# A hybrid mixer block: RWKV recurrence without GpSimd, retention and Mamba products on the full array, another order of issue

## The chip, the cores and the metric

The kernel runs on one core of a Trainium2 chip. The metric is device time in microseconds (us) of one execution; the median of three runs before the change is 1616.52 us (1614.81 to 1617.13).

## What is computed

One layer over 512 tokens and 1024 channels, in float32: `x = x + Mixer(RMSNorm(x))`, `x = x + ConvFFN(RMSNorm(x))`, and a last RMSNorm. The mixer projects the normed input once and feeds four token mixers (Mamba-2, RG-LRU, retention, RWKV-7), gates and projects each, sums them and projects the sum. The three parts that the change touches are, cut to their cores:

```
# RWKV-7, 16 heads of 64, one step per token
sk    = einsum('bhvk,bhk->bhv', state, kk_t)
state = state * w_t - sk * b_t + v_t * k_t
o_t   = einsum('bhvk,bhk->bhv', state, r_t)

# retention, 8 heads, qk width 64, v width 128, chunks of positions
scores  = einsum(q, k) * inner_decay
y_inner = einsum(scores, v)
kv      = einsum(k, v, decay_to_end)        # state that a chunk adds
y_cross = einsum(q * decay_from_start, previous_state)

# Mamba-2, per group of 4 heads
y_diag = einsum(cb * decay, xdt)
```

## The kernel before

Every large product is done three times: `split` cuts a float32 operand into a rounded part (`whi`, `hh`) on ScalarE and a rest (`wlo`, `hl`) on VectorE, and `mm3` (L118 to L121) adds hi*hi, lo*hi and hi*lo in PSUM. A weight block of 128x1024 comes by DMA (`wraw`), is split (`wsplit`), and `proj` or `proj_tokens` multiplies it with all 512 tokens. These blocks are the bulk of the work of TensorE. The small products inside the four mixers are plain float32 matmuls; TensorE does each of these as two passes, and the trace has a row for each pass.

RWKV goes in 8 blocks `j` of two heads. `rwkv_a1(j)` projects r, k and v and makes the decays `dx` and `di`. `rwkv_a2(j)` builds, for 8 chunks of 64 tokens, the stationary operands `g` and `bk` (L354 to L358), multiplies them (L372), masks the result into `g`, `gb` and `ab` (L374 to L376), scales `bk` by the chunk's decay (L381) and transposes it into `bt`, puts `v` into one half of `sv`, and inverts a triangular matrix by a loop of small VectorE operations (L424, L426), with several transfers through DRAM. `rwkv_b(j)` finishes the inverse `tt` (L452 to L465) and runs the recurrence over the 8 chunks:

```
sd = sv[h, c, e] * dl                      # L477, GpSimd, the decayed state
ps = g[c]^T sv[c]                          # L480
pp[c] = ps                                 # L482, VectorE
sk = tt[c]^T pp[c]                         # L484
sv[0:64, c, 0], sv[64:128, c, 1] = sk      # L485 ScalarE, L486 VectorE: solved rows over the state
sk[:, P:] = bt[c]^T sv[c]                  # L488
sv[h, c + 1, e] = sk[...] + sd             # L491, VectorE
```

After the chunks come the outputs (L497 to L501), the head norm (L504 to L517) and the gate; L524 makes the block's last result, which goes to DRAM as `y_dr[3][j]`.

The other three mixers are Python generators (`lru_tiles`, `ret_pair`, `mamba_group`), joined by `filler()` in the order `ORDER`, and behind them three of the four branch projections (`branch` with m = 1, 2, 0). The main loop calls `fill(24.0)` behind each `rwkv_a2(j)` and `fill(43.0)` behind each `rwkv_b(j)`: each takes steps of the generators until their stated us are used up. So a long chain of small RWKV steps stands between dense projections. Behind them come the RWKV branch (`branch(3, 3, merged)`, which needs all of `y_dr[3]`), the output projection and the FFN.

This order of the source is a priority only. The framework's scheduler lays down ahead of the run in which order each engine issues its instructions; it plays the program through a timing model, and an instruction of lower priority goes first where the model has it ready first. Each engine then issues in that fixed order and waits wherever the head of its queue is not ready. A pool with `bufs=n` hands out n buffers of a name; a further tile of that name waits until an older one is done with.

Of the kernel before, what the change touches and what calls it, by code (L numbers as in the profile page):

```python
# [63 lines left out]
def tile_hybrid_block(ctx, tc, x, wts, wzdt, lora, lruw, cpack, consts, rettab, nfin, out):  # L64
# [281 lines left out]
    def rwkv_a2(j, prep):  # L346
# [5 lines left out]
        for e in range(2):  # L352
            h = slice(64 * e, 64 * e + 64)
            nc.gpsimd.tensor_tensor(out=bk[h, :, 1 - e, :], in0=v3(k)[h], in1=v3(di)[h], op=ALU.mult)  # L354
            nc.vector.scalar_tensor_tensor(out=g[h, :, e, e, :], in0=v3(kk)[h], scalar=-1.0, in1=dx[h, :, 0:CH],
                                           op0=ALU.mult, op1=ALU.mult)
            nc.vector.scalar_tensor_tensor(out=bk[h, :, e, :], in0=v3(a)[h], scalar=0.5, in1=v3(di)[h], op0=ALU.mult, op1=ALU.mult)
            nc.gpsimd.tensor_tensor(out=g[h, :, e, 1 - e, :], in0=v3(r)[h], in1=dx[h, :, 1:], op=ALU.mult)  # L358
        nc.vector.scalar_tensor_tensor(out=r, in0=r, scalar=col("rwkv_r_k", j), in1=k, op0=ALU.mult, op1=ALU.mult)
# [20 lines left out]
        bkf = bk.rearrange("p c u t -> p c (u t)")  # L380
        nc.gpsimd.tensor_tensor(out=bkf, in0=bkf, in1=dl.unsqueeze(2).broadcast_to([P, NCH, P]), op=ALU.mult)  # L381
        bt = rkb.tile([P, NCH, P], F32, name="bt")
        for c4 in range(2):
# [3 lines left out]
            nc.scalar.copy(out=bt[:, 4 * c4:4 * c4 + 4, :], in_=ps.rearrange("p (c t) -> p c t", c=4))  # L387
        sv = rkb.tile([P, NCH, 2, 64], F32, name="sv")
        ps = ra.tile([P, S], F32, name="ra")
        for i in range(NT):  # L390
# [3 lines left out]
        for e in range(2):  # L394
            o = slice(64 - 64 * e, P - 64 * e)
            nc.scalar.copy(out=svv[o, :, 0, e], in_=pv[0:64, :, e])
            nc.vector.tensor_copy(out=svv[o, :, 1, e], in_=pv[64:128, :, e])


# [31 lines left out]
        for q in range(4):  # L431
            nc.sync.dma_start(out=xd[:, :, 8 * q:8 * q + 8], in_=xr[32 * q:32 * q + 16])
            nc.sync.dma_start(out=xtd.rearrange("b (m r) i -> b r m i", r=4)[:, q], in_=xt[32 * q:32 * q + 32])
        x11 = rkb.tile([P, NCH, 32], F32, name="x11")
        xtv = xtd.rearrange("(u q) c j -> u c q j", u=2)
        for e in range(2):
            b = 64 * e
            nc.sync.dma_start(out=x11[b:b + 32], in_=xd[8 * e:8 * e + 8].rearrange("q j c -> j q c"))
            for u in range(2):
                w = slice(b + 32 * u, b + 32 * u + 32)  # L440
                nc.sync.dma_start(out=tt[w, :, w], in_=xtv[u][:, 8 * e:8 * e + 8, :])
        return ab, x11, sv, bt, dl, bv

    def rwkv_b(j, held):
        ab, x11, sv, bt, dl, bv = held
        gh, gl = lora_x[2:]
# [20 lines left out]

        o = rkb.tile([P, NT, 2, 64], F32, name="o")
        pp = rkb.tile([P, NCH, 2, 64], F32, name="nt")
        for e in range(2):  # L470
            nc.gpsimd.memset(sv[64 * e:64 * e + 64, 0, e], 0.0)
        for c in range(NCH):
            if c < NCH - 1:
                sd = rkb.tile([P, 64], F32, name="sd", bufs=2)
                for e in range(2):
                    h = slice(64 * e, 64 * e + 64)
                    nc.gpsimd.tensor_scalar(out=sd[h], in0=sv[h, c, e], scalar1=dl[h, c:c + 1], scalar2=None, op0=ALU.mult)  # L477
            ps = rb.tile([P, S], F32, name="rb")
            for e in range(2):
                nc.tensor.matmul(ps[:, e * 64:(e + 1) * 64], g[:, c, e].rearrange("p u t -> p (u t)"), sv[:, c, e, :],  # L480
                                 start=True, stop=True)
            nc.vector.tensor_copy(out=pp[:, c], in_=ps[:, 0:P].rearrange("p (e v) -> p e v", e=2))  # L482
            sk = rb.tile([P, S], F32, name="rb")
            nc.tensor.matmul(sk[:, 0:P], tt[:, c, :], pp[:, c].rearrange("p e v -> p (e v)"), start=True, stop=True)  # L484
            nc.scalar.copy(out=sv[0:64, c, 0], in_=sk[0:64, 0:64])  # L485
            nc.vector.tensor_copy(out=sv[64:128, c, 1], in_=sk[64:128, 64:128])  # L486
            if c < NCH - 1:
                nc.tensor.matmul(sk[:, P:2 * P], bt[:, c, :], sv[:, c].rearrange("p e v -> p (e v)"), start=True, stop=True)  # L488
                for e in range(2):
                    h = slice(64 * e, 64 * e + 64)  # L490
                    nc.vector.tensor_tensor(out=sv[h, c + 1, e], in0=sk[h, P + 64 * e:P + 64 * e + 64], in1=sd[h], op=ALU.add)  # L491
        ppv = pp.rearrange("p (i o) e v -> p i o e v", o=2)
        for n in range(2):
            ps = rb.tile([P, S], F32, name="rb")
            for i in range(NT):
                c = 2 * i + n
                nc.tensor.matmul(ps[:, i * P:(i + 1) * P], gb[:, c, :], sv[:, c].rearrange("p e v -> p (e v)"), start=True, stop=True)  # L497
            pv = ps.rearrange("p (i e v) -> p i e v", i=NT, e=2)
            for e in range(2):
                h = slice(64 - 64 * e, P - 64 * e)  # L500
                nc.vector.tensor_tensor(out=o[64 * n:64 * n + 64, :, e], in0=pv[h, :, e], in1=ppv[h, :, n, e], op=ALU.add)  # L501
# [28 lines left out]
    def bg(shape):  # L530
        return fl.tile(shape, F32, name="bg", bufs=4)

# [77 lines left out]
    def ret_pair(j):  # L610
        q = sm([P, S])
        k = sm([P, S])
        for kind, t, sc in (("ret_q", q, 1.0), ("ret_k", k, 64.0 ** -0.5)):
            nc.scalar.activation(out=t, in_=proj(kind, j), func=AF.Copy, scale=sc)
# [4 lines left out]
            nc.vector.tensor_tensor(out=t, in0=t, in1=rope[0], op=ALU.mult)  # L619
            nc.vector.tensor_tensor(out=t, in0=t, in1=sw, op=ALU.add)  # L620
        vt = bg([P, NT, 256])

        def put(i, ps):
# [5 lines left out]
        tab = sm([P, S])  # L629
        nc.sync.dma_start(out=tab[:, 0:387], in_=rettab[j])  # L630
        qd = sm([P, NT, P])
        nc.vector.tensor_tensor(out=qd, in0=q.rearrange("p (i t) -> p i t", i=NT),
                                in1=tab[:, 256:384].unsqueeze(1).broadcast_to([P, NT, P]), op=ALU.mult)
        ps = inn.tile([P, S], F32, name="inn")
        for i in range(NT - 1):
            transpose(ps[:, i * P:(i + 1) * P], k[:, i * P:(i + 1) * P])
        kd = sm([P, NT, 2, 64])
        nc.vector.tensor_tensor(out=kd[:, 0:NT - 1], in0=ps[:, 0:384].rearrange("p (i e d) -> p i e d", i=NT - 1, e=2),
                                in1=tab[:, 384:386].unsqueeze(1).unsqueeze(3).broadcast_to([P, NT - 1, 2, 64]), op=ALU.mult)
        ps = inn.tile([P, S], F32, name="inn")  # L640
        for i in range(NT - 1):
            for e in range(2):
                nc.tensor.matmul(ps[64 * e:64 * e + 64, i * P:(i + 1) * P], kd[:, i, e, :], vt[:, i, e * P:(e + 1) * P],
                                 start=True, stop=True)
        kvs = sm([P, NT, P])
        nc.vector.tensor_copy(out=kvs[:, 0], in_=ps[:, 0:P])
        for i in range(1, NT - 1):
            nc.vector.scalar_tensor_tensor(out=kvs[:, i], in0=kvs[:, i - 1], scalar=tab[:, 386:387],
                                           in1=ps[:, i * P:(i + 1) * P], op0=ALU.mult, op1=ALU.add)
        for e in range(2):  # L650
            hd = 2 * j + e
            hs = slice(64 * e, 64 * e + 64)
            ps = inn.tile([P, S], F32, name="inn")
            for i in range(NT):
                w = slice(i * P, (i + 1) * P)
                nc.tensor.matmul(ps[:, w], k[hs, w], q[hs, w], start=True, stop=True)
            sc = sm([P, NT, P])
# [3 lines left out]
            for l in range(NT):  # L661
                w = slice(l * P, (l + 1) * P)
                nc.tensor.matmul(yp[:, w], sc[:, l, :], vt[:, l, e * P:(e + 1) * P], start=True, stop=l == 0)
                if l > 0:
                    nc.tensor.matmul(yp[:, w], qd[hs, l, :], kvs[hs, l - 1, :], start=False, stop=True)
            yv = yp.rearrange("p (l v) -> p l v", l=NT)
# [66 lines left out]
    def mamba_group(g):  # L733
# [52 lines left out]
        for i in range(NT):  # L786
            w = slice(i * P, (i + 1) * P)
            yp = inn.tile([P, S], F32, name="inn")
            for h in range(4):
                for u in range(2):  # L790
                    hs = slice(64 * u, 64 * u + 64)
                    nc.tensor.matmul(yp[hs, h * 64:(h + 1) * 64], mts[h][:, i, hs], xdt[:, i, h, :], start=True, stop=True)
            nc.vector.tensor_tensor(out=xs[:, i, :], in0=xs[:, i, :], in1=yp[:, 0:256], op=ALU.add)
# [258 lines left out]
def _shape_constants():  # L1052
# [19 lines left out]
    lg = np.log1p(-np.exp2(-5.0 - np.arange(8)))  # L1072
    tab = np.empty((4, P, 387), np.float64)
    keep = (i[None, :] // CH) >= (i[:, None] // CH)
    for j in range(4):
        for e in range(2):
            h = 2 * j + e
            tab[j, :, e * P:(e + 1) * P] = np.where(keep, np.exp(lg[h] * np.abs(i[None, :] - i[:, None])), 0.0)
            tab[j, 64 * e:64 * e + 64, 256:384] = np.exp(lg[h] * (i + 1.0))
            tab[j, :, 384 + e] = np.exp(lg[h] * (P - 1.0 - i))  # L1080
            tab[j, 64 * e:64 * e + 64, 386] = np.exp(lg[h] * P)
    tab = tab.astype(f)
# [93 lines left out]
```

## Time and profile before

| | |
|---|---|
| median of 3 runs | 1616.52 us (1614.81 to 1617.13) |
| the profiled execution, own time | 1615.14 us |
| its span, first to last instruction | 1613.4 us |
| TensorE busy | 1562.6 us (97%), 8452 matmul passes |
| VectorE, ScalarE, GpSimd busy | 1047.2, 719.7, 141.2 us |
| mean granted TensorE clock | 0.993 of full speed |

Matmuls are pipelined: a pass can start while the one before it is still leaving the array, so the durations of passes overlap, and what a pass costs is read from its start to the next start. A switch to another shape of the array is seen in the same way. PE is TensorE's matmul row, PEld its weight loads, DVE VectorE, ACT ScalarE, POOL GpSimd.

### The profile page before, as it was taken

What the parts mean: (1) busy time and instruction counts of PE and PEld (TensorE: products, weight loads), DVE (VectorE), ACT (ScalarE), POOL (GpSimd) and SP (SyncE); (2) the same over time, 40 slices, a digit from 0 to 9 for tenths busy, and PEclk for the clock granted to TensorE, in tenths of its full rate; (3) what the DMA queues carried; (4) which work ended last, traced back from release to release, by engine and by line L of the source; (5) the groups of instructions that cost most, each with busy time, mean ns of one, the idle gap of its engine ahead of it and who ended that gap; (6) DMA issues with size and microseconds to landing.
All of it is one profiled execution on the core that took longest, in us unless ns stands there. A gap on an engine that the chain in (4) does not pass through costs nothing.

```text
span 1613.4 us, 22510 instructions
## 1 busy us (share of the span) xinstructions
PE 1562.6 (97%) x8452; PEld 1279.7 (79%) x8452; DVE 1047.2 (65%) x2302; ACT 719.7 (45%) x1188; POOL 141.2 (9%) x190
## 2 busy tenths in 40 slices
PE   7899999899999999999999999999999999999998
PEld 7787778787788788877788778788888888888886
DVE  6787697875886788878636757544435665656233
ACT  6453466445753576258422432323223544444122
POOL 1200202202101201201200300100000000000000
PEclk9999999999999999999999999999999999999999
DMA  5233133232243234433533323444222223233231
GB/s 205 92 122 99 56 118 91 76 107 87 87 125 97 77 105 116 125 105 101 163 105 105 118 91 99 133 140 142 91 92 92 94 92 104 91 102 106 95 102 53
DMA packets 108461, 169.47 MB, mean 105 GB/s; under 512 B 54832, under 2 KB 64304, under 8 KB 108352
## 3 DMA queue, kind: packets, MB, share of 16 engines
q1 hardware_dynamic: 107632, 166.92, 33.0%
q8 instruction: 66, 1.08, 0.3%
q10 hardware_dynamic: 720, 1.11, 0.2%
q14 instruction: 43, 0.35, 0.1%
HBM read 150.66 MB, written 15.24 MB: 103 GB/s over the span
## 4 chain that ended last, share of the span: by engine, by line
PE 79%; DVE 14%; ACT 3%; issue 2%; POOL 1%; DMA 1%; SPq 0%; DVEq 0%; ACTq 0%; POOLq 0%
PE acc L119 17%; PE acc L120 17%; PE acc L121 17%; PE acc L949 3%; PE acc L951 3%; PE acc L950 3%; DVE wlo L101 2%; PE rb L480 2%; PE acc L242 2%; PE acc L241 2%; PE acc L240 2%; PE ra L372 1%; PE rb L488 1%; PE inn L96 1%; PE ra L96 1%
## 5 line engine op out<-in xcount | busy, mean ns | idle before, releaser
L119 PE MATMUL acc<-hh,whi 128*128 128x512 f32 (+1 forms) x1240 | 487.3, 393 | 0.0
L120 PE MATMUL acc<-hh,wlo 128*128 128x512 f32 (+1 forms) x1240 | 486.0, 392 | 1.2 <-DVE wlo L101 1.1
L121 PE MATMUL acc<-hl,whi 128*128 128x512 f32 (+1 forms) x1240 | 485.9, 392 | 0.0
L101 DVE TENSOR_TENSOR wlo<-raw,whi 128x1024 fp32r<-128x1024 f32 x228 | 279.1, 1225 | 169.7 <-ACT whi L100 168.8
L100 ACT CAST whi<-raw 128x1024 fp32r<-128x1024 f32 x228 | 237.8, 1045 | 205.9 <-PE acc L951 86.5
L120 PEld LDWEIGHTS acc<-hh,wlo 128*128 128x128 f32 x1240 | 234.3, 189 | 45.6 <-issue 2.2
L119 PEld LDWEIGHTS acc<-hh,whi 128*128 128x128 f32 x1240 | 234.3, 189 | 44.6 <-issue 2.2
L121 PEld LDWEIGHTS acc<-hl,whi 128*128 128x128 f32 x1240 | 234.2, 189 | 44.3 <-issue 1.8
L1004 DVE SCALAR_TENSOR_TENSOR fc<-acc,fw,fc 128x511 f32<-128x511 f32 x88 | 65.9, 749 | 76.5 <-ACT fc L1002 75.0
L119 PE MATMUL acc<-yh,whi 128*128 128x512 f32 x256 | 102.4, 400 | 0.0
L120 PE MATMUL acc<-yh,wlo 128*128 128x512 f32 x256 | 101.1, 395 | 0.0
L121 PE MATMUL acc<-yl,whi 128*128 128x512 f32 x256 | 100.9, 395 | 0.0
L477 POOL TENSOR_SCALAR sd<-sv,dl 64x64 f32<-64x64 f32 x112 | 57.4, 513 | 351.4 <-DVE sv L491 338.0
L1002 ACT ACTIVATE fc<-acc,fw 128x512 f32<-128x512 f32 x44 | 34.3, 779 | 93.9 <-PE acc L121 93.9
L240 PE MATMUL acc<-whi,hh 128*128 128x256 f32 (+1 forms) x256 | 74.8, 293 | 0.4 <-ACT whi L100 0.4
L241 PE MATMUL acc<-wlo,hh 128*128 128x256 f32 (+1 forms) x256 | 74.4, 291 | 0.0
L242 PE MATMUL acc<-whi,hl 128*128 128x256 f32 (+1 forms) x256 | 74.1, 290 | 0.0
L949 PE MATMUL acc<-whi,gh 128*128 128x512 f32 x176 | 69.4, 395 | 0.0
L951 PE MATMUL acc<-whi,gl 128*128 128x512 f32 x176 | 69.4, 395 | 0.0
L950 PE MATMUL acc<-wlo,gh 128*128 128x512 f32 x176 | 69.4, 395 | 0.0
L878 ACT ACTIVATE gt<-acc 128x512 f32<-128x512 f32 x32 | 19.0, 597 | 91.0 <-PE acc L121 91.0
L424 DVE TENSOR_TENSOR prod<-nt,xr 128x60 f32<-128x60 f32 (+24 forms) x248 | 54.0, 218 | 5.5
(329 smaller groups left out, 2404.8 us busy)
## 6 DMA issues: line engine op xcount, KB each, us to landing
raw<-in_wts_dram SPq DMA_DIRECT2D x226, 512.0 KB, 3.3
yr<-y SPq DMA_DIRECT2D x32, 256.0 KB, 2.8
y<-sm SPq DMA_DIRECT2D x24, 256.0 KB, 2.2
nt<-nd SPq DMA_DIRECT2D x32, 128.0 KB, 3.2
sm<-acd SPq DMA_DIRECT2D x16, 256.0 KB, 3.6
x<-in_x_dram SPq DMA_DIRECT2D x4, 512.0 KB, 5.3
ym<-bg SPq DMA_DIRECT2D x16, 128.0 KB, 1.8
sm<-sm SPq DMA_DIRECT2D x32, 64.0 KB, 2.0
```

The lines of the kernel that those rows point to most:

```text
L100: nc.scalar.copy(out=hi, in_=src)
L101: nc.vector.tensor_tensor(out=lo, in0=src, in1=hi.bitcast(F32), op=ALU.subtract)
L119: nc.tensor.matmul(ps, wh, xh, start=first, stop=False)
L120: nc.tensor.matmul(ps, wl, xh, start=False, stop=False)
L121: nc.tensor.matmul(ps, wh, xl, start=False, stop=last)
L240: nc.tensor.matmul(o, hh[:, ko, t], wh[:, s], start=ko == 0, stop=False)
L241: nc.tensor.matmul(o, hh[:, ko, t], wl[:, s], start=False, stop=False)
L242: nc.tensor.matmul(o, hl[:, ko, t], wh[:, s], start=False, stop=ko == KT - 1)
L949: nc.tensor.matmul(ps[i], xh[:, ko, t], w[0][:, s], start=ko == 0, stop=False)
L950: nc.tensor.matmul(ps[i], xh[:, ko, t], w[1][:, s], start=False, stop=False)
L951: nc.tensor.matmul(ps[i], xl[:, ko, t], w[0][:, s], start=False, stop=ko == 2 * nblk - 1)
L1004: nc.vector.scalar_tensor_tensor(out=t[:, s:], in0=ps[:, :S - s], scalar=fw[:, o + 2 - s:o + 3 - s], in1=t[:, s:], op0=ALU.mult, op1=ALU.add)
```

## The change

Recurrence: the solved rows and `v` go into a tile `uv` of their own, `v` being copied from `sv` by GpSimd; `sd` is gone, and the decay is fused into the addition on VectorE. Two multiplications of `rwkv_a2` (of `g` and of `bk`) move from GpSimd to VectorE. `x11` shares the buffer of `xr`, and `o` that of `ab`. Retention: `q` is laid out for both heads with zeros in the other head's 64 partitions (set by GpSimd), so that scores and cross terms contract over 128 partitions, and the keys `kd` are masked per head so that the chunk's state is accumulated by two matmuls of 128 columns. Mamba: two matmuls of 64 columns become one of 128. The pool of large tiles `bg` has 6 buffers in place of 4. The scheduler plays the program through another, finer timing model (`schedule_with_timeline_sim=True`), so the order of issue on every engine is laid down anew.

```
@@ rwkv_a2
-            nc.gpsimd.tensor_tensor(out=g[h, :, e, 1 - e, :], in0=v3(r)[h], in1=dx[h, :, 1:], op=ALU.mult)
+            nc.vector.tensor_tensor(out=g[h, :, e, 1 - e, :], in0=v3(r)[h], in1=dx[h, :, 1:], op=ALU.mult)
...
-        nc.gpsimd.tensor_tensor(out=bkf, in0=bkf, in1=dl.unsqueeze(2).broadcast_to([P, NCH, P]), op=ALU.mult)
+        nc.vector.tensor_tensor(out=bkf, in0=bkf, in1=dl.unsqueeze(2).broadcast_to([P, NCH, P]), op=ALU.mult)
...
+        uv = rkb.tile([P, NCH, 2, 64], F32, name="uv")
...
+            nc.gpsimd.tensor_copy(out=uv[o, :, e], in_=sv[o, :, e])
...
-        x11 = rkb.tile([P, NCH, 32], F32, name="x11")
+        x11 = rkb.tile([P, NCH, 32], F32, name="xr")
@@ rwkv_b
-        o = rkb.tile([P, NT, 2, 64], F32, name="o")
+        o = rkb.tile([P, NT, 2, 64], F32, name="ab")
...
-                sd = rkb.tile([P, 64], F32, name="sd", bufs=2)
-                for e in range(2):
-                    h = slice(64 * e, 64 * e + 64)
-                    nc.gpsimd.tensor_scalar(out=sd[h], in0=sv[h, c, e], scalar1=dl[h, c:c + 1], scalar2=None, op0=ALU.mult)
...
-            nc.scalar.copy(out=sv[0:64, c, 0], in_=sk[0:64, 0:64])
-            nc.vector.tensor_copy(out=sv[64:128, c, 1], in_=sk[64:128, 64:128])
+            nc.scalar.copy(out=uv[0:64, c, 0], in_=sk[0:64, 0:64])
+            nc.vector.tensor_copy(out=uv[64:128, c, 1], in_=sk[64:128, 64:128])
...
-                    nc.vector.tensor_tensor(out=sv[h, c + 1, e], in0=sk[h, P + 64 * e:P + 64 * e + 64], in1=sd[h], op=ALU.add)
+                    nc.vector.scalar_tensor_tensor(out=sv[h, c + 1, e], in0=sv[h, c, e], scalar=dl[h, c:c + 1],
+                                                   in1=sk[h, P + 64 * e:P + 64 * e + 64], op0=ALU.mult, op1=ALU.add)
@@ bg
-        return fl.tile(shape, F32, name="bg", bufs=4)
+        return fl.tile(shape, F32, name="bg", bufs=6)
@@ ret_pair
-        q = sm([P, S])
+        q = bg([P, 2, NT, P])
+        for e in range(2):
+            nc.gpsimd.memset(q[64 - 64 * e:P - 64 * e, e], 0.0)
...
-            nc.vector.tensor_tensor(out=t, in0=t, in1=sw, op=ALU.add)
+                nc.vector.tensor_tensor(out=k, in0=t, in1=sw, op=ALU.add)
+                for e in range(2):
+                    nc.vector.tensor_tensor(out=q[h, e].rearrange("p i t -> p (i t)"), in0=t[h], in1=sw[h], op=ALU.add)
...
-        kd = sm([P, NT, 2, 64])
+        kd = bg([P, 2, NT - 1, 2, 64])
...
-                nc.tensor.matmul(ps[64 * e:64 * e + 64, i * P:(i + 1) * P], kd[:, i, e, :], vt[:, i, e * P:(e + 1) * P],
-                                 start=True, stop=True)
+                nc.tensor.matmul(ps[:, i * P:(i + 1) * P], kd[:, e, i].rearrange("p f d -> p (f d)"), vt[:, i, e * P:(e + 1) * P],
+                                 start=e == 0, stop=e == 1)
...
-                nc.tensor.matmul(ps[:, w], k[hs, w], q[hs, w], start=True, stop=True)
+                nc.tensor.matmul(ps[:, w], k[:, w], q[:, e, i], start=True, stop=True)
...
-                    nc.tensor.matmul(yp[:, w], qd[hs, l, :], kvs[hs, l - 1, :], start=False, stop=True)
+                    nc.tensor.matmul(yp[:, w], qd[:, e, l], kvs[:, l - 1, :], start=False, stop=True)
@@ mamba_group
-                for u in range(2):
-                    hs = slice(64 * u, 64 * u + 64)
-                    nc.tensor.matmul(yp[hs, h * 64:(h + 1) * 64], mts[h][:, i, hs], xdt[:, i, h, :], start=True, stop=True)
+                nc.tensor.matmul(yp[:, h * 64:(h + 1) * 64], mts[h][:, i, :], xdt[:, i, h, :], start=True, stop=True)
@@ kernel
-    with _tile.TileContext(nc) as tc:
+    with _tile.TileContext(nc, schedule_with_timeline_sim=True) as tc:
```

`qd` likewise covers both heads in one operation over 128x1024, and `rettab` has 389 columns in place of 387 for the masks.

## Rows read from the trace of the kernel before

**Rows 1.** The page's busy time: us (share of the span) and instructions, by engine.
```profile
PE 1562.6 (97%) x8452; PEld 1279.7 (79%) x8452; DVE 1047.2 (65%) x2302; ACT 719.7 (45%) x1188; POOL 141.2 (9%) x190
```

**Rows 2.** Busy us by stretch: stretch, its length, then per engine; granted clock, DMA.
```profile
0.00:100.00 100.00, 83.73 (x487) 73.44 (x488) 72.58 (x178) 55.80 (x95) 14.23 (x17) 0.97 0.41 138
1100.00:1613.00 513.00, 505.94 (x2294) 418.08 (x2292) 254.63 (x339) 186.19 (x251) 0.00 (x0) 1.00 0.29 97
```

**Rows 3.** Waits of PE: who waited for whom, us in total, times, longest.
```profile
PE ra L372 <- DVE bk L357: 4.5, 1, 4.5
PE ra L96 <- POOL bk L381: 4.5, 4, 2.3
```

**Rows 4.** Timeline of PE, a burst of 128x128 float32 passes: start, us, what.
```profile
199.82 1.13 PE L372 MATMUL ra<-g,bk 128*128 128x128 f32 x8 [0.52 <-DVE gb L376]
200.71 0.48 PE L119 MATMUL acc<-hh,whi 128*128 128x512 f32 x1
...
201.02 0.40 PE L120 MATMUL acc<-hh,wlo 128*128 128x512 f32 x1
```

**Rows 5.** Timeline of PE, scores and outputs of one retention head.
```profile
702.79 0.39 PE L119 MATMUL acc<-hh,whi 128*128 128x512 f32 x1
703.11 1.16 PE L656 MATMUL inn<-sm 64*128 64x128 f32 x8
704.19 0.50 PE L120 MATMUL acc<-hh,wlo 128*128 128x512 f32 x1
704.53 0.39 PE L121 MATMUL acc<-hl,whi 128*128 128x512 f32 x1
704.76 0.40 PE L119 MATMUL acc<-hh,whi 128*128 128x512 f32 x1
...
705.46 0.61 PE L663 MATMUL inn<-bg,sm 128*128 128x128 f32 x4
...
708.07 0.50 PE L119 MATMUL acc<-hh,whi 128*128 128x512 f32 x1
```

**Rows 6.** Timeline of PE, the states of one retention pair.
```profile
149.55 0.88 PE L643 MATMUL inn<-bg,sm 128*64 128x128 f32 x12
150.36 0.50 PE L121 MATMUL acc<-hl,whi 128*128 128x512 f32 x1
150.69 0.40 PE L119 MATMUL acc<-hh,whi 128*128 128x512 f32 x1
```

**Rows 7.** Timeline of PE, one tile of a Mamba group.
```profile
137.61 0.28 PE L242 MATMUL acc<-whi,hl 128*128 128x256 f32 x1
137.82 0.69 PE L792 MATMUL inn<-bg,sm 128*64 128x64 f32 x16
138.43 0.39 PE L240 MATMUL acc<-whi,hh 128*128 128x256 f32 x1
138.65 0.28 PE L241 MATMUL acc<-wlo,hh 128*128 128x256 f32 x1
138.77 0.28 PE L242 MATMUL acc<-whi,hl 128*128 128x256 f32 x1
```

**Rows 8.** Groups of GpSimd's instructions: busy us, mean ns | idle before, releasers.
```profile
L477 POOL TENSOR_SCALAR sd<-sv,dl 64x64 f32<-64x64 f32 x112 | 57.4, 513 | 351.4 <-DVE sv L491 338.0 <-DVE dx L338 6.1 <-DVE dl L361 1.6
...
L358 POOL TENSOR_TENSOR g<-pr,dx 64x512 f32<-64x512 f32 x16 | 22.0, 1377 | 66.2 <-ACT dx L339 65.2
L381 POOL TENSOR_TENSOR bk<-bk,dl 128x1024 f32<-128x1024 f32 x8 | 16.0, 1996 | 180.0 <-PE ra L372 180.0
```

**Rows 9.** Timeline around the first hand-over of `ab` and `o`.
```profile
196.65 0.81 ACT L374 COPY ab<-ra 64x256 f32<-64x256 f32 x2
...
212.28 0.60 PE L96 MATMUL rb<-ident,o 128*128 128x128 f32 x4
```

**Rows 10.** Timeline of DVE: RWKV's last result; the third branch's last product.
```profile
1057.21 0.69 DVE L524 TENSOR_TENSOR yu<-yu,rb 128x512 f32<-128x512 f32 x1
...
1106.67 0.69 DVE L894 TENSOR_TENSOR gt<-acc,gt 128x512 f32<-128x512 f32 x1 [1.68 <-PE acc L121]
```

More of the change, by code (lines that the diff above doesn't have):

```diff
@@ L441, in rwkv_a2 @@
                 nc.sync.dma_start(out=tt[w, :, w], in_=xtv[u][:, 8 * e:8 * e + 8, :])
-        return ab, x11, sv, bt, dl, bv
+        return ab, x11, sv, uv, bt, dl, bv
     def rwkv_b(j, held):
-        ab, x11, sv, bt, dl, bv = held
+        ab, x11, sv, uv, bt, dl, bv = held
         gh, gl = lora_x[2:]
@@ L472, in rwkv_b @@
         for c in range(NCH):
-            if c < NCH - 1:
-                sd = rkb.tile([P, 64], F32, name="sd", bufs=2)
-                for e in range(2):
-                    h = slice(64 * e, 64 * e + 64)
-                    nc.gpsimd.tensor_scalar(out=sd[h], in0=sv[h, c, e], scalar1=dl[h, c:c + 1], scalar2=None, op0=ALU.mult)
             ps = rb.tile([P, S], F32, name="rb")
@@ L484, in rwkv_b @@
             nc.tensor.matmul(sk[:, 0:P], tt[:, c, :], pp[:, c].rearrange("p e v -> p (e v)"), start=True, stop=True)
-            nc.scalar.copy(out=sv[0:64, c, 0], in_=sk[0:64, 0:64])
-            nc.vector.tensor_copy(out=sv[64:128, c, 1], in_=sk[64:128, 64:128])
+            nc.scalar.copy(out=uv[0:64, c, 0], in_=sk[0:64, 0:64])
+            nc.vector.tensor_copy(out=uv[64:128, c, 1], in_=sk[64:128, 64:128])
             if c < NCH - 1:
-                nc.tensor.matmul(sk[:, P:2 * P], bt[:, c, :], sv[:, c].rearrange("p e v -> p (e v)"), start=True, stop=True)
+                nc.tensor.matmul(sk[:, P:2 * P], bt[:, c, :], uv[:, c].rearrange("p e v -> p (e v)"), start=True, stop=True)
                 for e in range(2):
                     h = slice(64 * e, 64 * e + 64)
-                    nc.vector.tensor_tensor(out=sv[h, c + 1, e], in0=sk[h, P + 64 * e:P + 64 * e + 64], in1=sd[h], op=ALU.add)
+                    nc.vector.scalar_tensor_tensor(out=sv[h, c + 1, e], in0=sv[h, c, e], scalar=dl[h, c:c + 1],
+                                                   in1=sk[h, P + 64 * e:P + 64 * e + 64], op0=ALU.mult, op1=ALU.add)
         ppv = pp.rearrange("p (i o) e v -> p i o e v", o=2)
@@ L496, in rwkv_b @@
                 c = 2 * i + n
-                nc.tensor.matmul(ps[:, i * P:(i + 1) * P], gb[:, c, :], sv[:, c].rearrange("p e v -> p (e v)"), start=True, stop=True)
+                nc.tensor.matmul(ps[:, i * P:(i + 1) * P], gb[:, c, :], uv[:, c].rearrange("p e v -> p (e v)"), start=True, stop=True)
             pv = ps.rearrange("p (i e v) -> p i e v", i=NT, e=2)
@@ L610, in ret_pair @@
     def ret_pair(j):
-        q = sm([P, S])
+        q = bg([P, 2, NT, P])
+        for e in range(2):
+            nc.gpsimd.memset(q[64 - 64 * e:P - 64 * e, e], 0.0)
         k = sm([P, S])
-        for kind, t, sc in (("ret_q", q, 1.0), ("ret_k", k, 64.0 ** -0.5)):
+        for kind, sc in (("ret_q", 1.0), ("ret_k", 64.0 ** -0.5)):
+            t = k if kind == "ret_k" else sm([P, S])
             nc.scalar.activation(out=t, in_=proj(kind, j), func=AF.Copy, scale=sc)
@@ L619, in ret_pair @@
             nc.vector.tensor_tensor(out=t, in0=t, in1=rope[0], op=ALU.mult)
-            nc.vector.tensor_tensor(out=t, in0=t, in1=sw, op=ALU.add)
+            if kind == "ret_k":
+                nc.vector.tensor_tensor(out=k, in0=t, in1=sw, op=ALU.add)
+            else:
+                for e in range(2):
+                    h = slice(64 * e, 64 * e + 64)
+                    nc.vector.tensor_tensor(out=q[h, e].rearrange("p i t -> p (i t)"), in0=t[h], in1=sw[h], op=ALU.add)
         vt = bg([P, NT, 256])
@@ L629, in ret_pair @@
         tab = sm([P, S])
[L630 to L633, printed above, removed]
+        nc.sync.dma_start(out=tab[:, 0:389], in_=rettab[j])
+        qd = bg([P, 2, NT, P])
+        nc.vector.tensor_tensor(out=qd.rearrange("p e i t -> p (e i) t"), in0=q.rearrange("p e i t -> p (e i) t"),
+                                in1=tab[:, 256:384].unsqueeze(1).broadcast_to([P, 2 * NT, P]), op=ALU.mult)
         ps = inn.tile([P, S], F32, name="inn")
@@ L636, in ret_pair @@
             transpose(ps[:, i * P:(i + 1) * P], k[:, i * P:(i + 1) * P])
-        kd = sm([P, NT, 2, 64])
-        nc.vector.tensor_tensor(out=kd[:, 0:NT - 1], in0=ps[:, 0:384].rearrange("p (i e d) -> p i e d", i=NT - 1, e=2),
-                                in1=tab[:, 384:386].unsqueeze(1).unsqueeze(3).broadcast_to([P, NT - 1, 2, 64]), op=ALU.mult)
+        kd = bg([P, 2, NT - 1, 2, 64])
+        for e in range(2):
+            nc.vector.tensor_tensor(out=kd[:, e], in0=ps[:, 0:384].rearrange("p (i f d) -> p i f d", i=NT - 1, f=2),
+                                    in1=tab[:, 384 + 2 * e:386 + 2 * e].unsqueeze(1).unsqueeze(3).broadcast_to([P, NT - 1, 2, 64]),
+                                    op=ALU.mult)
         ps = inn.tile([P, S], F32, name="inn")
@@ L647, in ret_pair @@
         for i in range(1, NT - 1):
-            nc.vector.scalar_tensor_tensor(out=kvs[:, i], in0=kvs[:, i - 1], scalar=tab[:, 386:387],
+            nc.vector.scalar_tensor_tensor(out=kvs[:, i], in0=kvs[:, i - 1], scalar=tab[:, 388:389],
                                            in1=ps[:, i * P:(i + 1) * P], op0=ALU.mult, op1=ALU.add)
@@ L651, in ret_pair @@
             hd = 2 * j + e
-            hs = slice(64 * e, 64 * e + 64)
             ps = inn.tile([P, S], F32, name="inn")
@@ L1072, in _shape_constants @@
     lg = np.log1p(-np.exp2(-5.0 - np.arange(8)))
-    tab = np.empty((4, P, 387), np.float64)
+    tab = np.zeros((4, P, 389), np.float64)
     keep = (i[None, :] // CH) >= (i[:, None] // CH)
@@ L1079, in _shape_constants @@
             tab[j, 64 * e:64 * e + 64, 256:384] = np.exp(lg[h] * (i + 1.0))
-            tab[j, :, 384 + e] = np.exp(lg[h] * (P - 1.0 - i))
-            tab[j, 64 * e:64 * e + 64, 386] = np.exp(lg[h] * P)
+            tab[j, :, 384 + 3 * e] = np.exp(lg[h] * (P - 1.0 - i))
+            tab[j, 64 * e:64 * e + 64, 388] = np.exp(lg[h] * P)
     tab = tab.astype(f)
```

## The prediction

> **What bounds the kernel.** I read the busy times first: TensorE (PE) is busy 97% of the span [rows 1], VectorE 65%, GpSimd 9%. So a microsecond counts only where PE issues or waits. Its idle time is 1613.4 - 1562.6 = 50.8 us. The stretches say where: 100 - 83.7 = 16.3 us in the first 100 us, where PE also waits for its first operands, and 513 - 505.9 = 7.1 us in everything after 1100 us, where only dense products are left [rows 2]. That leaves 50.8 - 16.3 - 7.1 = 27.4 us between 100 and 1100 us, where RWKV's chains run between the dense blocks. The waits of PE name the causes: VectorE's `bk` for L372 (4.5 us, once), GpSimd's `bk` of L381 for the transposes (4.5 us in four) [rows 3], and a tail of short ones. The reader is to see two things in the timeline. Where nothing disturbs, a 128x512 pass follows another after 704.76 - 704.53 = 0.23 us, while its own record lasts 0.39 to 0.40 [rows 5]: a gap of up to 0.17 us is hidden in "busy", so the 50.8 us are not all the loss. And where the form of the stationary operand changes, the starts move apart.
>
> **The retention and Mamba matmuls.** These are on PE, so each term counts fully, where filling matmuls stand on both sides. A burst of eight full 128x128 float32 passes costs 200.71 - 199.82 = 0.89 us and delays the next dense pass by 201.02 - 200.71 - 0.23 = 0.08 [rows 4]; a pass more or less in a burst is 0.89 / 8 = 0.11.
>
> - Scores (L656, eight passes of 64x128 per head): from 702.79 to 703.11 is 0.32, 0.09 over the usual 0.23; the burst is 704.19 - 703.11 = 1.08; the dense pass behind it takes 0.34, 0.11 over [rows 5]. Together 1.28. On the full array 0.89 + 0.08 = 0.97. Saved 0.31, eight heads: 2.5 us.
> - Outputs (L663 full, L665 of 64 rows, alternating, 14 passes per head): 708.07 - 705.46 = 2.61, and 0.11 behind it as above: 2.72 [rows 5]. With one form, 14 passes are 0.89 + 6 x 0.11 = 1.55, and 0.08 behind: 1.63. Saved 1.09, eight heads: 8.7 us.
> - States (L643, 12 passes of 128x64, two column halves side by side): 150.36 - 149.55 = 0.81 and 150.69 - 150.36 - 0.23 = 0.11 behind, and 0.09 ahead as for the scores: 1.01 [rows 6]. After: 12 full passes, 0.89 + 4 x 0.11 + 0.08 = 1.41. Lost 0.40, four pairs: 1.6 us.
> - Mamba (L792, 16 passes of 128x64): 0.61, with 0.09 ahead (137.82 - 137.61 = 0.21 against 0.12 for a 256-column pass) and 0.10 behind: 0.80 [rows 7]. After: 8 full passes over 64 columns; the trace has no such burst of eight, so at most 0.97 as with 128 columns [rows 4], at least today's 0.80, since half as many matmuls save nothing in a pair that already runs side by side. 0 to 0.17, 16 tiles: 0 to 2.7 us lost; I take 1.3.
>
> Sum on PE: -2.5 - 8.7 + 1.6 + 1.3 = -8.3 us, with Mamba's bounds -9.6 to -6.9.
>
> Here a rule bears the other way. Packed halves really overlap in this trace: twelve half passes take 0.81 us, 0.07 each, where a full pass takes 0.11 [rows 4, 6]. The 64-row passes don't: eight take 1.08, 0.13 each [rows 5]. The Trainium skill, "TensorEngine Tiling (Array Packing)", sections "Theoretical Speedup" and "When to Use Tiling", advises the opposite of this edit: a contraction or an output of 64 or less should be packed, for up to twice the speed. By that page all four sites would slow down, up to twofold. The trace bears it out for the column halves, and not for the row halves.
>
> **VectorE and GpSimd.** GpSimd is not late in the recurrence: it sits idle 338.0 us for VectorE's `sv` ahead of `sd` [rows 8], has one operation of 0.51 us to do, and its result is needed only after three matmuls and their copies. Taking away L477 (57.4 us of GpSimd) therefore gives nothing directly. The fused operation in its place has the same size as L491's; I cost it at 0. VectorE gets 16 multiplications for `g` of 512 columns and 8 for `bk` of 1024; at 0.69 for 512 columns, as L524 takes [rows 10], that is 11.0 + 11.0; retention adds one more 512-column sum, 512 more columns of `qd` and 384 more of `kd` per pair, 4 x (0.69 + 0.69 + 0.52) = 7.6. Together 30 us on an engine that has 566 us idle: 0 if covered, 30 if every one became a wait of PE. For `bk` the operation itself gets shorter, 2.00 to about 1.4, four of whose waits were worth 4.5 us; but it now queues behind whatever VectorE holds, the splits of weights among it, and the transposes of L96, `bt` and the recurrence wait for it. I set the two against each other: 0. GpSimd's new copies into `uv`, 16 at no more than L358's 1.38 us [rows 8], are 22 us on an engine that loses 95, ahead of a long inversion: 0, the cover being that inversion.
>
> **Shared buffers.** `ab` of the next block can't be written before `o` of the last has been transposed. In the first hand-over ScalarE writes `ab` at 196.65, while the transposes of `o` come at 212.28 [rows 9]: 15.6 us that would have to be waited out. Nothing on PE waits for it while filling work is left. RWKV's last result comes at 1057.2 and the third branch's last product at 1106.7 [rows 10]: 49.5 us of cover before the RWKV branch has to wait. 0, unless the chain gets later by more than that: seven hand-overs of 7 us each.
>
> **Order of issue.** No row shows a better or worse order; it is a new program order on all engines. From below: it helps at most by the idle time between 100 and 1100 us, some of the first 100 us and as much again hidden in the 0.17 us overlaps, say 45 us as an estimate from [rows 2, 5]. From above: it could make PE wait as much again as now between 100 and 1100 us, 27 us. Queues are fixed, so PE waits now because a matmul was placed where the model thought its operand ready; the gap of 4.5 us for L372 is such a misplacement [rows 3]. A model closer to the durations misplaces less. I take about half of the visible 27.4 and a little of the first 100 us: -16.
>
> **Sum.** Against the profiled execution's own 1615.1: -8.3 - 16 = 1590.8. The median of the runs is 1.4 us above that execution, so **1592 us**.
>
> **Rivals.**
>
> - Likeliest, 0.48: as above, 1592, its own range 1578 to 1604.
> - The order removes most waits, 0.18: -8.3 - 42 from 1616.5, 1566. For it: nearly all of the loss sits in one region with dense work at hand. Against: some waits are chain latency at the start.
> - The order does nothing, only the matmuls' form counts, 0.15: 1616.5 - 8.3 = 1608, and up to the old time where VectorE's 30 us bite a little; half of this is within 0.2%.
> - Slower, 0.16: RWKV is pushed behind the filling work. The place is `branch(3, 3, merged)`, the price PE standing idle, the point from which it decides 49.5 us of delay. With the first hand-over's 15.6 us at four more places, 78 us of delay, 28 of them uncovered: 1616.5 - 8 + 28 = 1636. For it: shared buffers, 30 us more on VectorE in that chain, a new order. Against: rows 9 show the earliest hand-over, at which the filling work was fresh, and a scheduler that sees the shared buffer pulls the tail of the block ahead.
> - Packing lost, 0.03: the full form costs at all four sites what the half passes saved there. If row halves went side by side as column halves do, 112 passes of 64 rows would go from 0.07 to 0.11 (4.5 us), with the 1.6 and 2.7 above: 1616.5 + 9 = 1625 with nothing from the order. The trace is against it: 0.13 per row-half pass. That is the price by rows of what the Trainium skill's packing advice implies.
>
> 0.2% of the time, some 3.2 us, is about what can be told from no change. Faster: 0.48 + 0.18 + 0.08 = 0.74. Same: 0.07. Slower: 0.16 + 0.03 = 0.19. The range, from the strong rival up to where the slower one begins in earnest: 1564 to 1622; beyond it lie some 1 in 10 on either side.
>
> **What would show each step.** Retention: L656, L665 and L663 all 128*128, 14 output passes from first start to the next dense start in about 1.55 us instead of 2.61, and the pass behind a burst of scores at 0.31 instead of 0.34. States: 12 passes in 1.3 instead of 0.81. Mamba: 8 passes in 0.8 to 0.9. VectorE busy near 1077 us, GpSimd near 70. Order: PE's idle time in the stretch 100 to 1100 down from 27 to about 14, with the `bk` waits shorter; L524's last start before the third branch's last product. The prediction is wrong if that idle time stays or grows, if the granted clock drops in more stretches than before, or if L524 ends behind L894's third branch.

## The result and the profile after

The changed kernel takes **1849.9 us** (median of 4 runs, 1849.0 to 1850.6) against 1616.3 of before: a ratio of 1.145, 95% interval 1.143 to 1.147. It is slower by 14.5%, and 228 us above the range.

The page of after, busy us (share of the span) and instructions by engine, then two lines in 40 slices, as tenths: PE's busy share and its granted clock:

```profile
span 1848.2 us, 22146 instructions
PE 1630.6 (88%) x8324; PEld 1353.5 (73%) x8324; DVE 1079.1 (58%) x2334; ACT 725.9 (39%) x1190; POOL 59.9 (3%) x78
...
PE   7998889888879778968999899995569999999998
...
PEclk9998889999979888978999899997579999999999
```

Against [rows 1], VectorE (1079) and GpSimd (60) stand near where they were forecast (1077 and 70), and PE has 128 matmul passes fewer, but it is idle for 1848.2 - 1630.6 = 217.6 us instead of 50.8, and busy for 68 us more. The span's growth, 234.8, is 166.8 of idle time and 68.0 of "busy" time. The granted clock has digits below 9 only where PE's busy digits fall too. The clock's records in the trace put 184 us of the busy time at the lower of its two levels (1.2 GHz of 2.4), 18 before; at 0.43 us per dense pass in place of 0.23 (rows further down) that is about 77 us more, an estimate, so the clock can account for the longer busy time.

The stretches of after, with columns as in [rows 2]:

```profile
0.00:100.00 100.00, 86.12 (x503) 75.87 (x504) 70.01 (x174) 59.88 (x96) 8.10 (x14) 1.00 0.38 136
100.00:1100.00 1000.00, 866.97 (x4676) 720.42 (x4675) 649.82 (x1575) 429.41 (x759) 45.04 (x56) 0.91 0.29 89
1100.00:1240.00 140.00, 140.00 (x698) 115.80 (x697) 64.30 (x98) 46.24 (x67) 3.40 (x2) 1.00 0.36 117
1240.00:1360.00 120.00, 61.34 (x304) 48.51 (x302) 54.43 (x167) 14.19 (x33) 3.35 (x6) 0.62 0.13 35
1360.00:1848.00 488.00, 476.14 (x2150) 392.94 (x2150) 240.50 (x323) 176.23 (x237) 0.00 (x0) 0.99 0.29 96
```

The middle stretch of the kernel before, for comparison:

```profile
100.00:1100.00 1000.00, 972.95 (x5675) 788.18 (x5674) 719.95 (x1786) 477.70 (x843) 126.97 (x173) 0.99 0.35 106
```

The start and the dense tail are as before. Between 100 and 1100 us PE gets 999 passes fewer done (at most 128 of them because the new forms need fewer), with 133 us idle instead of 27 and a clock of 0.91. From 1240 to 1360 it does half a stretch's work at 0.62: nothing is left to fill with. The timeline of after, VectorE, shows the two ends that [rows 10] show before:

```profile
1231.43 0.69 DVE L900 TENSOR_TENSOR gt<-acc,gt 128x512 f32<-128x512 f32 x1 [1.98 <-PE acc L121]
...
1354.27 0.69 DVE L522 TENSOR_TENSOR yu<-yu,rb 128x512 f32<-128x512 f32 x1
```

RWKV's last result now comes 123 us behind the third branch's last product, where it came 49.5 ahead. All three signs of being wrong that the prediction names are there: the idle time grew, the clock dropped in more stretches, and this. PE's waits of after:

```profile
PE rb L454 <- DMA xr<-xd: 34.8, 7, 24.5
PE rb L485 <- DVE uv L483: 21.9, 24, 3.9
...
PE rb L481 <- DVE nt L479: 13.5, 25, 1.8
...
PE rb L477 <- DVE sv L488: 11.5, 28, 0.7
```

L477, L481 and L485 are the three matmuls of a step of the recurrence, and L454 belongs to the inversion ahead of it: part of the chain is in the open. These four are 82 of the 218 us; the rest is in many other groups, waits of the filling work among them. That doesn't yet say why. From the starts and ends in the trace I worked out how long each of the eight recurrences lasts, from its first matmul (L480, after: L477) to its last solved rows: 34 us on the mean before, 69 us after. The eight of after are not alike. The seventh runs from the first line here to the end of the second:

```profile
1121.81 0.66 PE L477 MATMUL rb<-sv,g 128*128 128x64 f32 x4
...
1252.60 0.23 DVE L483 COPY uv<-rb 64x64 f32<-64x64 f32 x1 [1.35 <-ACT uv L482]
```

That is 131 us, most of it in the stretch 1100 to 1240, where PE is never idle and has its full clock. The eighth lies in 1240 to 1360, has no filling beside it, and lasts 31 us, no longer than before.

### The profile page after: what moved, and what is told of

It is laid out like the page before. It is cut to its first block, busy times and chain, and to the rows that moved or that the text cites. A ratio compares the mean times of both kernels' runs of the same rounds, so it can differ in the third digit from the quotient of the medians.

```text
span 1848.2 us, 22146 instructions
## 1 busy us (share of the span) xinstructions
PE 1630.6 (88%) x8324; PEld 1353.5 (73%) x8324; DVE 1079.1 (58%) x2334; ACT 725.9 (39%) x1190; POOL 59.9 (3%) x78
## 4 chain that ended last, share of the span: by engine, by line
PE 62%; DVE 9%; ACT 5%; DMA 3%; issue 2%; SPq 1%; DVEq 0%; ACTq 0%
PE acc L119 14%; PE acc L120 14%; PE acc L121 14%; PE acc L955 3%; PE acc L957 3%; PE acc L956 3%; PE rb L477 1%; DVE wlo L101 1%; PE ra L372 1%; PE rb L481 1%; PE rb L485 1%; DVE prod L426 1%; DVE xr L428 1%; ACT whi L100 1%; PE acc L240 1%
## 5 line engine op out<-in xcount | busy, mean ns | idle before, releaser
L119 PEld LDWEIGHTS acc<-hh,whi 128*128 128x128 f32 x1240 | 240.2, 194 | 82.1 <-ACT sm L689 16.6
L120 PEld LDWEIGHTS acc<-hh,wlo 128*128 128x128 f32 x1240 | 240.2, 194 | 47.0 <-issue 1.0
L121 PEld LDWEIGHTS acc<-hl,whi 128*128 128x128 f32 x1240 | 238.5, 193 | 48.3 <-issue 1.0
L1010 DVE SCALAR_TENSOR_TENSOR fc<-acc,fw,fc 128x511 f32<-128x511 f32 (+1 forms) x88 | 65.8, 749 | 75.5 <-ACT fc L1008 74.0
L426 DVE TENSOR_TENSOR prod<-nt,xr 128x60 f32<-128x60 f32 (+24 forms) x248 | 58.1, 234 | 18.5 <-DMA nt<-nd 13.7
L119 PEld LDWEIGHTS acc<-yh,whi 128*128 128x128 f32 x256 | 49.0, 192 | 20.6 <-ACT yh L100 10.6
L559 DVE SCALAR_TENSOR_TENSOR sm<-acc,cp,sm 128x511 f32<-128x511 f32 (+2 forms) x72 | 52.9, 744 | 15.7 <-ACT sm L557 15.2
```

The source lines that it names most:

```text
L119: nc.tensor.matmul(ps, wh, xh, start=first, stop=False)
L120: nc.tensor.matmul(ps, wl, xh, start=False, stop=False)
L121: nc.tensor.matmul(ps, wh, xl, start=False, stop=last)
L426: nc.vector.tensor_tensor(out=pr[:, 0:n, 0:m], in0=nt[:, jj, jj + 1:32].unsqueeze(2).broadcast_to([P, n, m]), in1=xr[:, jj:jj + 1, 0:m].br ...
```

## Experiments

Each run stands beside runs of the kernel before (1616 to 1618). In the diffs, `+` is the experiment's.

**1 and 2: code and order apart.** All edits with the old order; and before with nothing but the new order.

```
e1 (from after)   -    with _tile.TileContext(nc, schedule_with_timeline_sim=True) as tc:
                  +    with _tile.TileContext(nc) as tc:
e2 (from before)  -    with _tile.TileContext(nc) as tc:
                  +    with _tile.TileContext(nc, schedule_with_timeline_sim=True) as tc:
```

> All edits of the change, but the order of issue laid down by the old timing model. Theory T1 (the new order itself stretches RWKV's recurrence from 36 to some 70 us per block and pushes it behind the filling work): back to about 1608 us, that is the old time less the 8 us of the matmul forms. Theory T2 (the shared buffer of ab and o serialises the blocks whatever the order): 1750 to 1850 us. Rival T3 (30 us more work on VectorE): 1630 to 1650 us.

> The kernel before with nothing changed but the timing model that lays down the order. T1: about 1840 us, like the changed kernel. T2: 1580 to 1616 us. T3: no slower than before.

Measured: e1 1603.5 (ratio 0.991, 0.988 to 0.993); e2 1824.8 (1.128, 1.126 to 1.130). So the code's edits gain 13 us under the old order, and the order alone costs 208. Of the three theories only T1 has both. Stretches of e2:

```profile
100.00:1100.00 1000.00, 883.77 (x4903) 725.20 (x4902) 641.33 (x1562) 436.14 (x773) 112.39 (x141) 0.90 0.29 90
...
1230.00:1330.00 100.00, 59.81 (x304) 47.60 (x303) 48.35 (x156) 15.12 (x33) 8.80 (x17) 0.68 0.18 47
```

The same picture as after: a thin middle, then a block with nothing beside it. Its recurrences last 79 us on the mean, e1's 34; its last one, with nothing beside it, 32.

**3 and 4: the shared buffer, under each order.** `o` in `ab`'s buffer in the kernel before; and a buffer of its own in after, with one buffer fewer for `yr`, a tile of the branches, to make room.

```
e3 (from before)  +        o = rkb.tile([P, NT, 2, 64], F32, name="ab")
e4 (from after)   +        o = rkb.tile([P, NT, 2, 64], F32, name="o")
                  +            yr = bp.tile([P, S], F32, name="yr", bufs=1)
```

> The kernel before, old order model, with one edit: o takes the buffer of ab. T1: 1616 to 1630 us. T2: 1700 us or more, each hand-over adding some 6 us behind the transposes of o and the block's loop of 114 us becoming the period. T3: 1616 us.

> The changed kernel with a buffer of its own for o; to make room, yr in the branch projections has one buffer in place of two. T1: about 1840 us. T2: about 1600 us, with ab written before the transposes of the old o again. T3: 1630 to 1650 us.

Measured: e3 1616.9 (0.999, 0.998 to 1.001), e4 1793.7 (1.110, 1.106 to 1.113). The sharing costs nothing under the old order and 1849.9 - 1793.7 = 56 us under the new one (the one `yr` buffer fewer may cost e4 something on top, which no run separates). For e4 that is between the 1840 and the 1600 that were expected. The first hand-over of after, timeline, VectorE, PE and ScalarE:

```profile
256.85 0.69 DVE L512 TENSOR_TENSOR ab<-ab,orsr 128x512 f32<-128x512 f32 x1
...
262.60 0.60 PE L96 MATMUL rb<-ident,ab 128*128 128x128 f32 x4
...
265.09 0.75 ACT L374 COPY ab<-ra 64x256 f32<-64x256 f32 x2
```

The next block's `ab` is written right behind the transposes of `o`, and in all seven hand-overs 3 to 8 us after the start of L512: the blocks are strung end to end. In [rows 9] `ab` was ahead of them, but that is the first hand-over. The third of before, timeline, VectorE and ScalarE, and the first of e3:

```profile
430.85 0.69 DVE L514 TENSOR_TENSOR o<-o,orsr 128x512 f32<-128x512 f32 x1
...
439.47 0.76 ACT L374 COPY ab<-ra 64x256 f32<-64x256 f32 x2
```
```profile
206.20 0.69 DVE L514 TENSOR_TENSOR ab<-ab,orsr 128x512 f32<-128x512 f32 x1
...
209.50 0.75 ACT L374 COPY ab<-ra 64x256 f32<-64x256 f32 x2
```

From the third hand-over on, before writes `ab` 8 to 25 us behind L514 with buffers of their own, so that only two hand-overs had anything to wait for; e3 strings its blocks in the same way and loses nothing. In e2 `ab` comes 13 to 19 us ahead of L514 in all seven, and in e4 ahead of L512 in all seven. So under the new order every hand-over has a lead that the shared buffer takes away, under the old one only the first two.

**5, 6 and 9: the edits one by one, old order.** e5: retention, Mamba and the `bg` buffers alone. e6: the RWKV edits alone. e9: e1 with the two column-half forms kept.

```
e9 (from e1)  -  nc.tensor.matmul(yp[:, h * 64:(h + 1) * 64], mts[h][:, i, :], xdt[:, i, h, :], ...)
              +  for u in range(2):
              +      hs = slice(64 * u, 64 * u + 64)
              +      nc.tensor.matmul(yp[hs, h * 64:(h + 1) * 64], mts[h][:, i, hs], xdt[:, i, h, :], ...)
              (and the states' matmuls over kd[:, i, e, :] in the same way)
```

> The kernel before with the retention and Mamba edits alone (full array, six bg buffers), old order model, old RWKV. By the prediction's terms: 8.3 us less than before, 1608 us; with Mamba's bounds 1607 to 1610. If the 13 us that all edits gain under the old order come from RWKV's edits instead: 1616 us.

> The kernel before with the RWKV edits alone (uv, the fused operation, two multiplications on VectorE, the shared buffers), old order model. By the prediction's terms: 0, 1616 us. If taking GpSimd out of the chain matters: 1605 to 1611 us. If VectorE's 22 us in RWKV bite: 1620 us or more.

> All edits of the change under the old order model, but the column halves kept where they ran side by side: retention's states (L643) and Mamba (L792) as in the kernel before. By the prediction's terms, 1.6 and 1.3 us less than with all edits under the old order (1603.5): 1600 us, with Mamba's bounds 1599 to 1602. If packing lost nothing at these sites: 1603 us or above.

Measured: e5 1610.6 (0.996, 0.994 to 0.997), e6 1615.6 (0.999, 0.998 to 1.000), e9 1605.4 (0.992, 0.991 to 0.993). So e5's 7 us belong to the matmul forms and the two further `bg` buffers together, which no run separates; the RWKV edits show no effect by themselves; keeping the halves, expected to gain, can't be told from e1. The new forms in e1's timeline, PE: scores and outputs of a head, and a Mamba tile:

```profile
696.09 0.39 PE L120 MATMUL acc<-hh,wlo 128*128 128x512 f32 x1
696.32 1.05 PE L664 MATMUL inn<-bg,sm 128*128 128x128 f32 x8
697.13 0.48 PE L121 MATMUL acc<-hl,whi 128*128 128x512 f32 x1
697.45 0.40 PE L119 MATMUL acc<-hh,whi 128*128 128x512 f32 x1
...
698.57 0.71 PE L671 MATMUL inn<-bg,sm 128*128 128x128 f32 x4
699.12 0.39 PE L673 MATMUL inn<-sm,bg 128*128 128x128 f32 x2
...
700.15 0.48 PE L120 MATMUL acc<-hh,wlo 128*128 128x512 f32 x1
700.47 0.40 PE L121 MATMUL acc<-hl,whi 128*128 128x512 f32 x1
```

```profile
654.44 1.06 PE L798 MATMUL inn<-bg,sm 128*128 128x64 f32 x8
655.31 0.36 PE L242 MATMUL acc<-whi,hl 128*128 128x256 f32 x1
655.51 0.28 PE L240 MATMUL acc<-whi,hh 128*128 128x256 f32 x1
```

**7: what the new order puts into the chain.** In the kernel before, a ready matmul of the chain starts almost at once (timeline, around one L484):

```profile
385.80 0.29 DVE L482 COPY nt<-rb 128x128 f32<-128x128 f32 x1
385.89 0.39 PE L119 MATMUL acc<-hh,whi 128*128 128x512 f32 x1
386.12 0.39 PE L120 MATMUL acc<-hh,wlo 128*128 128x512 f32 x1
386.35 0.38 PE L484 MATMUL rb<-nt,tt 128*128 128x128 f32 x2
```

The same place in e2: the copy ends at 172.49, and the matmul that needs it starts 4.28 us later, behind a run of dense passes of which the first and the last are shown:

```profile
172.20 0.29 DVE L482 COPY nt<-rb 128x128 f32<-128x128 f32 x1 [4.13 <-PE rb L480]
...
172.45 0.40 PE L119 MATMUL acc<-hh,whi 128*128 128x512 f32 x1
...
176.54 0.39 PE L119 MATMUL acc<-hh,whi 128*128 128x512 f32 x1
176.77 0.38 PE L484 MATMUL rb<-nt,tt 128*128 128x128 f32 x2
```

Counted from the starts in the trace, over all steps: from the operand's end to the start of L484, L488 and L480 it takes 0.43, 0.28 and -0.05 us on the mean before (L480 starts with one head's half of the state, ahead of the other's), and 2.26, 2.09 and 1.33 in e2, with 9, 9 and 6 PE passes in between in place of 3, 1 and 0. The three places grew by 1.83, 1.81 and 1.38 us; with eight of the first and seven of each other per recurrence that is 37 of the 45 us by which a recurrence grew. This wait appears in no list of PE's waits as far as PE is busy meanwhile. e7 splits each dense pass of e2 into two of 256 columns, to ask whether a number of passes or a time is put there:

```
+        for c0 in (0, 256):
+            w = slice(c0, c0 + 256)
             for ko in range(KT):
+                mm3(ps[:, w], wh[:, s], wl[:, s], hh[:, ko, w], hl[:, ko, w], ko == 0, ko == KT - 1)
```

> The kernel before with the new order model, and the dense projections cut into passes of 256 columns, twice as many of half the length. Theory Q (the new model lays a fixed number of passes ahead of a chain's matmul that has become ready): some 10 passes between still, so half the time, and a recurrence of about 55 us per block in place of 79; the time falls towards 1720 to 1780 us though the passes themselves are a little dearer. Theory B (a whole projection block goes ahead of the chain): 20 passes between, the recurrence stays at 79 us, and the time at 1825 us or above.

Measured (one run): 1784.4, recurrence 74 us; over the three places 1.8 us and 12 passes on the mean, where e2 has 1.9 us and 8. A fixed number of passes falls; it is nearer a fixed time, but neither theory holds as stated, and the time of 1784 lies between theirs. What in the finer model puts the passes there stays open.

**8, 10 and 11: why a longer recurrence costs the kernel time.** After each block's two parts, dense work worth a fixed amount by the program's own estimates is emitted (`FILL`). If that amount is fixed, a chain longer than it can cover leaves PE empty. e8 and e10 halve the filling, under the new and the old order; e11 makes the chain longer under the old order, with eight needless multiplications by 1.0 per step.

```
e8, e10  -FILL = (24.0, 43.0)
         +FILL = (12.0, 21.5)
e11      +            for _ in range(8):
         +                nc.gpsimd.tensor_scalar(out=sv[:, c], in0=sv[:, c], scalar1=1.0, scalar2=None, op0=ALU.mult)
```

> The kernel before with the new order model and half the filling work between the RWKV steps (12 and 21.5 in place of 24 and 43), so that RWKV has priority over more of the dense work. Theory P (the filling work goes ahead because it has the higher priority): the recurrence falls back towards 35 to 50 us per block and the time to 1650 to 1700 us. Theory Q (passes laid ahead whatever the priority): the recurrence stays at 65 us or more, and the time above 1750 us.

> The kernel before, old order model, with half the filling work between the RWKV steps. If the loss with half the filling (1861 us under the new model) is one of the new model: the old one pulls later dense work ahead and stays within 1610 to 1660 us. If half the filling starves TensorE whatever the model: 1750 us or more, and the run with half the filling says nothing of the model.

> The kernel before, old order model, with eight multiplications of the state by 1.0 on the idle GpSimd at the head of each recurrence step, one behind the other: the recurrence gets some 5 us longer per step, 40 to 45 per block, with no dense work moved and the values unchanged. Theory C (the length of RWKV's chain against a fixed amount of filling work per block sets the time; that is what the new order spoils): the period of a block goes from 127 to about 155 us and the time to 1750 to 1830 us, with the granted clock down to 0.92 to 0.95. Theory W (the new order loses by waits at the head of TensorE's queue all over, and a longer chain alone is hidden): 1616 to 1650 us.

Measured, one run each: e8 1860.7, e10 1773.2, e11 1958.6. The same stretch, 100 to 1100 us, of e8, of e10, and of e11, with e11's longest wait in the recurrence:

```profile
100.00:1100.00 1000.00, 829.15 (x4625) 673.68 (x4624) 639.78 (x1687) 408.37 (x760) 133.80 (x174) 0.83 0.25 75
```
```profile
100.00:1100.00 1000.00, 883.63 (x4987) 709.83 (x4986) 673.49 (x1721) 425.06 (x782) 122.06 (x173) 0.90 0.29 87
```
```profile
100.00:1100.00 1000.00, 809.67 (x4361) 655.26 (x4360) 573.37 (x1429) 396.75 (x715) 340.20 (x515) 0.88 0.25 76
```
```profile
PE rb L482 <- POOL sv L479: 220.9, 55, 6.6
```

e11 reproduces after's picture with the old order: its recurrences last 89 us instead of 34, from the first matmul of one to that of the next it takes 164 us instead of 122 (e2: 158; means of seven), and the clock falls to 0.88. The difference is that its wait is PE's own and stands in the list of waits. 55 us in each of eight blocks, 437 us, cost 342; the expectation had the direction and not the size. At that rate e2's 361 us of longer recurrences would cost some 280, an estimate: more than its 208, so their length is enough to explain the loss. How much of it comes from PE's waits elsewhere was not separated. e10 shows that too little filling alone does the same: 156 us lost with recurrences of 35 us, so that e8's time by itself says little of the new order. e8 is a mixed answer: the recurrences fall from 79 to 49 us, as they should if filling passes stretch them, but halved filling costs more than that gives back, so the time doesn't fall. At halved filling the new order is still 88 us worse than the old.

## Why the prediction was wrong, point by point

- **Order of issue** (forecast -16, bounds -45 to +27): the step that failed. Alone it costs 208 us (e2), on top of the other edits 1849.9 - 1603.5 = 246. The bounds were taken from the idle time that PE had before, as if an order could only move PE's own waits. What it moved was the chain: dense passes ahead of ready matmuls stretch each recurrence from 34 to 79 us, under filling that is fixed per block. "A model closer to the durations misplaces less" was an argument without a row; no run shows which model is closer, and the order of the finer one cost time.
- **The slower rival** (1636 us, chance 0.16) named the place, `branch(3, 3, merged)`, and the sign. Its price, 28 us, covered only the hand-overs, at 15.6 us each; that figure is the first hand-over's, and before has no such lead from the third on. In the changed kernel PE does stand beside RWKV's last block, as this rival has it; what it lacked is the idle time in the earlier blocks (133 us against 27 between 100 and 1100 us) and the clock.
- **The clock.** Below 1.0 in the stretches where PE stands: 0.90 to 0.91 in the middle and 0.62 in after's unfilled block. Of the chip's two levels, 1.2 and 2.4 GHz, part of the time then goes at the lower. The prediction named a drop of the clock as a sign of being wrong and gave it no price. In e2's timeline PE stands 3.44 us, then 3.85, and the next dense passes come at about half pace, 0.42 to 0.43 apart, until 0.23 returns:

```profile
651.39 0.49 PE L484 MATMUL rb<-nt,tt 128*128 128x128 f32 x2 [3.44 <-DVE nt L482]
...
658.63 0.80 PE L119 MATMUL acc<-hh,whi 128*128 128x512 f32 x1 [3.85 <-ACT sm L604]
659.23 0.63 PE L120 MATMUL acc<-hh,wlo 128*128 128x512 f32 x1
659.65 0.63 PE L121 MATMUL acc<-hl,whi 128*128 128x512 f32 x1
...
662.63 0.39 PE L119 MATMUL acc<-hh,whi 128*128 128x512 f32 x1
662.86 0.40 PE L120 MATMUL acc<-hh,wlo 128*128 128x512 f32 x1
```

- **Shared buffers** (0, "unless the chain gets later"): 0 under the old order (e3), 56 us under the new (e4), where the cover of 49.5 us is gone. The condition came true; in the sum it was a clause, and the one case that held it was the slower rival with its 28 us.
- **Form of the matmuls** (-8.3): right, e5 gives -7 (interval -9 to -5). The run has the `bg` buffers too, but the terms as measured in e1 add up to about -8 by themselves. By term, in e1's rows above: 14 output passes 700.15 - 698.57 = 1.58 (forecast 1.55); scores 697.13 - 696.32 = 0.81 and the pass behind at 0.32 (0.89 and 0.31); Mamba 655.31 - 654.44 = 0.87, and 655.51 - 655.31 = 0.20 behind it (0.8 to 0.9); 12 state passes, in the burst of e1 at 673.5 us, 1.26 (1.33). Whether the two column-half sites lose the forecast 3 us, e9 can't resolve. The Trainium skill, "TensorEngine Tiling (Array Packing)", "When to Use Tiling", advises tiling for a contraction or an output of 64 or less. The gain of e5 doesn't test that: the 64-row passes of a head all read the same 64 partitions (`k[hs, w]`), so at these sites the kernel before never ran two row halves side by side. For the scores and the outputs, then, neither the prediction's "all four sites would slow down" nor its reading that the trace is against packing follows; no run here packs them there.
- **VectorE and GpSimd** (0): right for the RWKV edits alone, e6 0.999. Of the up to 30 us more on VectorE nothing shows under the old order: e1, with all of them, is faster than before.
- **The 13 us of e1** are more than e5's 7 and e6's 1 to 2 together; nothing run here separates the rest.

What stays open: what in the finer model places some 2 us of dense work ahead of a ready matmul of the chain. The version that beats both kernels is e1, all the edits with the old order: 0.991 of before; e9, at 0.992, can't be told from it.

## What to carry to other kernels

A change of the order of issue is a change of its own: time it alone before anything is put beside it, since here it hid a gain of 13 us under a loss of 246. Where a serial chain runs under a fixed amount of filling, look at the time from "operand ready" to "matmul starts": the engine is busy meanwhile, so no list of its waits has it, and every microsecond there is multiplied by the steps of the chain. A buffer shared at no cost is shared at no cost only under the order that was measured.

## What the runs showed of the hardware

Where PE's work gets thin, the clock is lower as well: e10, e11 and e8, with PE idle for 12, 19 and 17% of 100 to 1100 us, show 0.90, 0.88 and 0.83, where 3% idle showed 0.99. It doesn't go by the idle share alone: e11 is idle most and e8 has the lowest clock. And a 64-row pass of one row group, 0.13 in [rows 5], is slower than the full pass in its place, 0.81 / 8 = 0.10.
